# Handing rotary rotations over later, moving one table operation, and evicting the attention's values by two engines

## The chip, the cores and the metric

The kernel runs on one core of a Trainium2 chip. The metric is device microseconds of one execution. Three runs of the kernel before gave 1201.23, 1202.62 and 1203.34 us, a median of 1202.62 us. The core's engines are called PE (matrix products; its weight loads are the rows PEld), DVE (vector), ACT (scalar), POOL and SP. SP issues all transfers of this kernel, in the order in which they stand in its queue.

## The reference

The program is a two-layer encoder over 256 tokens of width 2048. Each layer normalises x, multiplies it by one wide input matrix, and feeds two groups of heads: a bidirectional recurrent scan (16 heads of 64) and an attention limited to a band of 128 tokens (16 query heads, 4 key and value heads) whose queries and keys are rotated by position. Each group is gated, the results are concatenated, multiplied by an output matrix and added to x. A last normalisation follows. The part that the change touches is the rotation, the tables for it and the values:

```python
proj = jnp.einsum('btd,dc->btc', rms_norm(x, norm_g[l]), w_in[l])
rw_in, g_rw, q, k_at, v_at, g_at = jnp.split(proj, col_splits, axis=-1)
qh, kh = rope(q, positions), rope(k_at, positions)   # t1*cos - t2*sin, t2*cos + t1*sin
y_at = window_attention(qh, kh, v_at, sink[l])        # softmax over the band and a sink
y_rw = rwkv7_branch(...)                              # one scan per direction
x = x + jnp.concatenate([y_rw * silu(g_rw), y_at * silu(g_at)], -1) @ w_out[l]
```

## The kernel before, in words

Every large product is a list of tiles of 128 output columns. A tile takes 16 **steps**, each of three products of 128x128 by 128x256 (L291 to L293), because every float32 operand is split in a high and a low part. The weights come as two halves of 512 KB per tile: SP loads one (`raw`, three buffers), ACT rounds it to the high part (`hi`, L221) and DVE subtracts that to get the low part (`lo`, L223).

The steps of all tiles stand in one queue, `Stream`. A `window` is a stretch of 64 steps (four tiles), cut in 14 slots; at chosen slots pieces of other work are put between the steps: the recurrent scan of head pairs (stages `scan_p`, `scan_i` and `scan_b`), in layer 0 the pieces of `setup` that compute the rotary tables COS and SIN, and from the eleventh window on the pieces of the attention. `S.later(n, f)` emits f when n more steps have been emitted. PE's instructions stand in exactly the order in which they are emitted. For the other engines a scheduler sets the order from dependences and priorities (`tc.high_priority` moves work forward); what is issued through `PA` and `PV` keeps its program order. Once set, each engine works through its list in order, so an instruction that waits holds back everything behind it. The helper through which `PA` and `PV` record shows as L236.

Each layer runs eight windows of scan inputs. Then, in the ninth, come 32 steps for the attention's values (`pva`, L560 to L562, two accumulators for the two halves of the tokens) and the two key tiles k0 and k1; in the tenth the query tiles q0 to q3, one after the other; in the next two the remaining four queries alternate with gate tiles. The names k0 to q7 are used below.

`rope_evac` follows every key and query tile. ACT copies the accumulator to `u` (L532). SP issues four small transfers of 32 rows (L534) that write the swapped halves to `rrot`, of which there is a single buffer. Seven steps on, `turn` gives DVE three operations: u times the cosine table, rrot times the sine table, and their sum into u. The first of these writes u, which the four transfers read, so it waits for them. Ten steps on, `parts` lets ACT write the rounded high part (from `u`) and DVE the rest.

`v_evac` scales the two accumulators of the values into `VA` with two DVE operations (L569). The accumulators stand in the two buffers that the next tiles use, so the first product of k0 waits for the first one.

The scan's triangular inverse, `scan_i`, passes between engines at each level: PE writes `pq`, ACT copies to `QF` (L900) and to `tt` (L868), PE writes `pd` (L906), DVE merges it into `tv` (L907), and PE goes on (L897, at the end L864 into `pf`). `scan_b` carries the state: PE writes `pcc` (L954 to L977), ACT evicts to `rh` (L956) and `suv` (L972), DVE scales `suv` (L979).

Of the kernel before, what the change touches and what calls it, by code (L numbers as in the profile page):

```python
# [15 lines left out]
AF = mybir.ActivationFunctionType  # L16
ALU = mybir.AluOpType
# [38 lines left out]
ROT = {0: [2, 3], 1: [], 7: [3, 6, 9], 8: [1, 4], 9: []}  # L56
PRIO_B = 95
# [76 lines left out]
def hybrid_trunk_kernel(ctx, tc, xT, wi, wv, wo, par, fing, dup, iup, sink, pos, cst, out):  # L134
    nc = tc.nc
    V, A, G, PE, SY = nc.vector, nc.scalar, nc.gpsimd, nc.tensor, nc.sync
# [22 lines left out]
    def st(tag, shape, dt=F32, bufs=1):  # L159
        return sp.tile([128, *shape], dt, tag=tag, name=tag, bufs=bufs)  # L160
# [114 lines left out]
    S = Stream()  # L275
# [117 lines left out]
    def window(n, *gens, groups=SLOTS):  # L393

        done = 0
        for i in range(groups):
            for g, at in gens:
                for _ in range(at.count(i)):
                    if g.__name__ == "scan_b":
                        with tc.high_priority(offset=PRIO_B):  # L400
                            next(g, None)
                    else:
                        next(g, None)
            upto = n * (i + 1) // groups
            S.run(upto - done)
            done = upto
# [5 lines left out]
    for l in range(DEPTH):  # L412
        L = Layer()
# [7 lines left out]
    def queue_inputs(l):  # L421
        L = layers[l]
# [100 lines left out]
        def rope_evac(place):  # L523
            def evac(pm):
                if not rope:
                    rope.extend((st("TW", [T]), st("XA", [T])))
                    V.tensor_tensor(rope[0], COS, L.norm.rb, op=ALU.mult)
                    V.tensor_tensor(rope[1], SIN, L.norm.rb, op=ALU.mult)
                CR, SR = rope
                raw = st("u", [T], bufs=2)  # L530
                rot = st("rrot", [T])
                A.activation(raw, pm, AF.Copy)  # L532
                for q in range(4):
                    SY.dma_start(out=rot[q * 32 : q * 32 + 32, :], in_=raw[(q ^ 1) * 32 : (q ^ 1) * 32 + 32, :])  # L534
                hi, lo = place()

                def turn():
                    PV.tensor_tensor(raw, raw, CR, op=ALU.mult)
                    PV.tensor_tensor(rot, rot, SR, op=ALU.mult)
                    PV.tensor_tensor(raw, raw, rot, op=ALU.add)  # L540

                def parts():
                    PA.activation(hi, raw, AF.Copy)
                    PV.tensor_tensor(lo, raw, hi.bitcast(F32), op=ALU.subtract)

                S.later(7, turn)
                S.later(10, parts)

            return evac

        pvs = []
# [13 lines left out]

        def v_evac():
            L.VA = st("VA", [2, 256])
            for b in range(2):
                V.tensor_scalar(L.VA[:, b, :], pvs[b], L.norm.rt[:, b : b + 1], None, op0=ALU.mult)  # L569

        for qt in range(4):
            S.add(
# [80 lines left out]
    def layer(l):  # L653
        L = layers[l]
# [363 lines left out]
        def scans(w):  # L1018

            gens = []  # L1020
            prep = [(w, STAGE_P0[w])] if w < 2 else [(2, STAGE_P[1]), (1, STAGE_P[0])]
            stages = [(lag, scan_p, at[0]) for lag, at in prep]
            stages += [(4, scan_b, STAGE_B[1]), (3, scan_i, STAGE_I[1]), (3, scan_b, STAGE_B[0])]
            stages += [(2, scan_i, STAGE_I[0])]
            stages += [(lag, scan_p, at[1]) for lag, at in prep]
            for lag, scan, at in stages:
                p = w - lag
                if 0 <= p < NP:
                    if (scan, p) not in chains:
                        chains[scan, p] = scan(p, L.ts[p])  # L1030
                    gens.append((chains[scan, p], at))
            return gens
# [57 lines left out]
        def attend():  # L1090

            scores(0)
            yield
            flip(0)
            scores(1)
            yield
            for j in range(8):
                values(j)
                if j < 6:
                    scores(j + 2)  # L1100
                yield
                if j < 7:
                    flip(j + 1)
                    yield

        for w in range(NP + 2):
            window(64, *scans(w), *([(setup_, ROT.get(w, [3, 6, 9, 12]))] if l == 0 else []))
        att = attend()
        window(64, *scans(NP + 2), (att, ATT[0]))
        window(64, *scans(NP + 3), (att, ATT[1]))  # L1110
# [32 lines left out]
    setup_ = setup()  # L1143
    next(setup_)
    S.run(8)
    for l in range(DEPTH):
        queue_output(l)
        if l + 1 < DEPTH:
            queue_inputs(l + 1)
        layer(l)  # L1150
        S.run(NKT * 16)
        if l + 1 < DEPTH:
            S.run(32)
# [89 lines left out]
```

## Time and profile before

| | |
|---|---|
| runs | 1201.23, 1202.62, 1203.34 us; median 1202.62 |
| profiled execution, its own time | 1201.32 us |
| its span, first to last instruction | 1199.5 us |
| PE busy / PEld busy | 1165.4 / 1087.2 us |
| DVE busy / ACT busy | 910.2 / 776.3 us |
| mean granted PE clock | 0.991 of full |
| values and k0 start in layer 0 / layer 1 | about 340 / 926 us |
| rotations in layer 0 / layer 1 | 353 to 484 / 940 to 1069 us |

How to read it. A row of waits names the engine and line that waited, what it waited for, the total in us, the number of waits and the longest. In a timeline row stand the start, the length, the engine, line and tiles, and in brackets the idle time of the engine before it and what ended that. Successive products of PE overlap, so a product shows 0.28 us while it is issued every 0.12 us. In a row of a stretch of time stand the busy time of each engine with its number of instructions, the granted PE clock, and the transfer share.

### The profile page before, as it was taken

What the parts mean: (1) busy time and instruction counts of PE and PEld (TensorE: products, weight loads), DVE (VectorE), ACT (ScalarE), POOL (GpSimd) and SP (SyncE); (2) the same over time, 40 slices, a digit from 0 to 9 for tenths busy, and PEclk for the clock granted to TensorE, in tenths of its full rate; (3) what the DMA queues carried; (4) which work ended last, traced back from release to release, by engine and by line L of the source; (5) the groups of instructions that cost most, each with busy time, mean ns of one, the idle gap of its engine ahead of it and who ended that gap; (6) DMA issues with size and microseconds to landing.
All of it is one profiled execution on the core that took longest, in us unless ns stands there. A gap on an engine that the chain in (4) does not pass through costs nothing. (4 is left out here: it accounts for less than half of the span.)

```text
span 1199.5 us, 38085 instructions
## 1 busy us (share of the span) xinstructions
PE 1165.4 (97%) x16151; PEld 1087.2 (91%) x16151; DVE 910.2 (76%) x2019; ACT 776.3 (65%) x1953; POOL 18.9 (2%) x23
## 2 busy tenths in 40 slices
PE   8999999999999999999999999999999999999996
PEld 6998999999888889999999989999998888889996
DVE  6888888888876668866667978887887766786554
ACT  6666776777776557655555766876777665665553
POOL 0000000000000000000000000000000000000000
PEclk8999999999999999999999999999999999999998
DMA  7553333323333434467655443334323333345653
GB/s 254 163 174 124 107 100 114 118 85 115 110 105 106 129 98 137 143 221 249 214 183 166 133 129 113 100 106 127 115 92 99 116 115 131 113 148 186 212 186 121
DMA packets 60410, 166.63 MB, mean 139 GB/s; under 512 B 7728, under 2 KB 22736, under 8 KB 60240
## 3 DMA queue, kind: packets, MB, share of 16 engines
q1 hardware_dynamic: 60240, 164.21, 42.5%
q8 instruction: 126, 2.06, 0.7%
q14 instruction: 44, 0.36, 0.1%
HBM read 157.37 MB, written 4.19 MB: 135 GB/s over the span
## 5 line engine op out<-in xcount | busy, mean ns | idle before, releaser
L291 PE MATMUL pm<-XH,hi 128*128 128x256 f32 x1664 | 495.9, 298 | 3.4 <-ACT XH L183 1.7
L293 PE MATMUL pm<-XH,lo 128*128 128x256 f32 x1664 | 469.9, 282 | 6.2 <-DVE lo L223 6.2
L292 PE MATMUL pm<-XL,hi 128*128 128x256 f32 x1664 | 469.4, 282 | 0.3
L221 ACT ACTIVATE hi<-raw 128x512 fp32r<-128x512 f32 x560 | 327.7, 624 | 194.9 <-PE pm L292 110.3
L223 DVE TENSOR_TENSOR lo<-raw,hi 128x512 fp32r<-128x512 f32 x560 | 369.7, 686 | 97.5 <-ACT hi L221 91.3
L291 PEld LDWEIGHTS pm<-XH,hi 128*128 128x128 f32 x1664 | 315.0, 189 | 18.5 <-ACT XH L183 2.4
L293 PEld LDWEIGHTS pm<-XH,lo 128*128 128x128 f32 x1664 | 315.4, 190 | 8.8 <-DVE lo L223 8.5
L292 PEld LDWEIGHTS pm<-XL,hi 128*128 128x128 f32 x1664 | 315.4, 190 | 1.1 <-DVE XL L184 1.1
L291 PE MATMUL pm<-MH,hi 128*128 128x256 f32 x512 | 144.1, 281 | 0.0
L293 PE MATMUL pm<-MH,lo 128*128 128x256 f32 x512 | 144.0, 281 | 0.0
L292 PE MATMUL pm<-ML,hi 128*128 128x256 f32 x512 | 143.8, 281 | 0.0
L291 PEld LDWEIGHTS pm<-MH,hi 128*128 128x128 f32 x512 | 96.6, 189 | 0.8 <-issue 0.8
L293 PEld LDWEIGHTS pm<-MH,lo 128*128 128x128 f32 x512 | 96.6, 189 | 0.2 <-DVE lo L223 0.2
L292 PEld LDWEIGHTS pm<-ML,hi 128*128 128x128 f32 x512 | 96.6, 189 | 0.0
L907 DVE CAST_PREDICATED tv<-LV,pd 128x256 f16<-128x256 uint8 x80 | 34.4, 430 | 12.8 <-PE pd L906 12.2
L790 DVE TENSOR_TENSOR ge<-pg,C 128x1024 f32<-128x1024 f32 x32 | 38.9, 1221 | 4.4 <-PE pg L784 4.4
L972 ACT ACTIVATE suv<-pcc 64x128 f32<-64x128 f32 x128 | 34.2, 267 | 11.4 <-PE pcc L970 7.1
L900 ACT ACTIVATE QF<-pq 128x256 f16<-128x256 f32 x80 | 30.8, 384 | 14.3 <-PE pq L864 13.8
L1062 ACT ACTIVATE mv<-mv,mx 128x257 f32<-128x257 f32 x64 | 31.8, 501 | 11.3 <-DVE mx L1059 11.3
L956 ACT ACTIVATE rh<-pcc 128x128 f32<-128x128 f32 x64 | 17.5, 273 | 33.2 <-PE pcc L954 32.8
L784 PE MATMUL pg<-mv,bk 64*128 64x128 f32 x512 | 37.2, 285 | 0.3 <-DVE ge L790 0.3
L784 PEld LDWEIGHTS pg<-mv,bk 64*128 64x128 f32 x512 | 31.1, 187 | 2.4 <-DVE ge L790 0.4
(247 smaller groups left out, 1860.1 us busy)
## 6 DMA issues: line engine op xcount, KB each, us to landing
raw<-wi SPq DMA_DIRECT2D x207, 512.0 KB, 3.8
raw<-wo SPq DMA_DIRECT2D x64, 512.0 KB, 4.2
raw<-wv SPq DMA_DIRECT2D x8, 512.0 KB, 3.7
rrot<-u SPq DMA_DIRECT2D x80, 32.0 KB, 2.1
vg<-xT SPq DMA_DIRECT2D x16, 128.0 KB, 4.2
xd<-vg SPq DMA_DIRECT2D x16, 128.0 KB, 3.5
vg<-xd SPq DMA_DIRECT2D x16, 128.0 KB, 3.7
g<-dup SPq DMA_DIRECT2D x16, 97.0 KB
```

What stands on the lines that cost most here:

```text
L221: A.activation(hi[:, q], raw[:, q], AF.Copy)
L223: V.tensor_tensor(lo[:, q], raw[:, q], hi[:, q].bitcast(F32), op=ALU.subtract)
L291: PE.matmul(pm, wh, rh[:, kk, :], start=(kk == 0), stop=False)
L292: PE.matmul(pm, wh, rl[:, kk, :], start=False, stop=False)
L293: PE.matmul(pm, wl, rh[:, kk, :], start=False, stop=(kk == 15))
L784: PE.matmul(pg[:, h, c * 128 : (c + 1) * 128], BK[half[h], d, c, 1 - h : 3 - h, :].rearrange("p s j -> p (s j)"), MV[half[h], d, c].rearra ...
L790: V.tensor_tensor(GEd(d), pg.rearrange("p h (c x) -> p h c x", c=NC), gm[d].unsqueeze(1).unsqueeze(1).to_broadcast([128, 2, NC, 128]), op= ...
L900: A.activation(t_sub(QF), flat4(pq[:, :, 0:128]), AF.Copy)
L907: V.copy_predicated(t_sub(TC), t_mask, flat4(pd[:, :, 0:128]))
L956: A.activation(RH, pc[:, 0], AF.Copy)
L972: A.activation(here(h), pc[half[h], 1], AF.Copy)
L1062: A.activation(Sc[:, h, q, 0:257], Sc[:, h, q, 0:257], AF.Exp, scale=0.125, bias=mx[:, q : q + 1], accum_out=den[:, q : q + 1])
```

## The change

Three places are edited. The rotation of a tile is handed over 13 steps after its eviction instead of 7, and its rounding 15 steps after instead of 10. In the third to the seventh window of layer 0, the third of four pieces of `setup` moves from slot 9 to slot 12, where the fourth stands as well. `v_evac` gives the first accumulator to ACT and the second to DVE, both at raised priority.

```diff
-                S.later(7, turn)
-                S.later(10, parts)
+                S.later(13, turn)
+                S.later(15, parts)
...
         def v_evac():
             L.VA = st("VA", [2, 256])
-            for b in range(2):
-                V.tensor_scalar(L.VA[:, b, :], pvs[b], L.norm.rt[:, b : b + 1], None, op0=ALU.mult)
+            with tc.high_priority(offset=PRIO_B):
+                A.activation(L.VA[:, 0, :], pvs[0], AF.Copy, scale=L.norm.rt[:, 0:1])
+                V.tensor_scalar(L.VA[:, 1, :], pvs[1], L.norm.rt[:, 1:2], None, op0=ALU.mult)
...
         for w in range(NP + 2):
-            window(64, *scans(w), *([(setup_, ROT.get(w, [3, 6, 9, 12]))] if l == 0 else []))
+            window(64, *scans(w), *([(setup_, ROT.get(w, [3, 6, 12, 12]))] if l == 0 else []))
```

The order of PE's instructions and of POOL's is the same before and after; the orders of DVE, ACT and SP differ. One line is added in `v_evac`, so lines behind it count one more in the kernel after (L907 becomes L908).

The first place is DVE in the tenth window of layer 0, where q0 and q1 are rotated (`u` and `rrot` with the tables, which lie in `TW` and `XA`). Before:

```order
L907 COPY_PREDICATED tv<-LV,pd 128x2x64x2
L236 TENSOR_TENSOR u<-u,TW 128x256
L236 TENSOR_TENSOR rrot<-rrot,XA 128x256
L223 TENSOR_TENSOR lo<-raw,hi 128x512
L236 TENSOR_TENSOR u<-u,rrot 128x256
L979 TENSOR_TENSOR suv<-pcc,pc 64x2x64 x2
L236 TENSOR_TENSOR iu<-u,kr 128x256
L223 TENSOR_TENSOR lo<-raw,hi 128x512 x2
L907 COPY_PREDICATED tv<-LV,pd 128x2x32x4
```

and after:

```order
L908 COPY_PREDICATED tv<-LV,pd 128x2x64x2
L223 TENSOR_TENSOR lo<-raw,hi 128x512 x2
L980 TENSOR_TENSOR suv<-pcc,pc 64x2x64 x2
L236 TENSOR_TENSOR u<-u,TW 128x256
L236 TENSOR_TENSOR rrot<-rrot,XA 128x256
L236 TENSOR_TENSOR u<-u,rrot 128x256
L236 TENSOR_TENSOR iu<-u,kr 128x256
L223 TENSOR_TENSOR lo<-raw,hi 128x512
L908 COPY_PREDICATED tv<-LV,pd 128x2x32x4
```

Two of the low parts and the scaling of `suv` now stand ahead of the rotation of q0, and the low part of the query (`iu`) directly behind it.

The second place is ACT where the values end in layer 0. Before:

```order
L236 ACTIVATE pp<-lw 128x512
L956 ACTIVATE rh<-pcc 128x128
L236 ACTIVATE ip<-lw 128x512
```

and after:

```order
L236 ACTIVATE pp<-lw 128x512
L569 ACTIVATE VA<-pva,rt 128x256
L957 ACTIVATE rh<-pcc 128x128
L236 ACTIVATE ip<-lw 128x512
```

The eviction of the first accumulator stands on ACT between `pp` and `rh`; on DVE one of the two evictions is gone and the other keeps its place behind the reciprocal of `kd`.

The third place is SP's queue at the transfers of q0. The first row ends with what it waits for; before it is

```order
L534 DMA rrot_7367<-u_7366 32x256 [waits DMAHW3_49,DMAHW2_49,DMAHW4_49,DMAHW1_49,Activation_49]
L534 DMA rrot_7367<-u_7366 32x256 [waits DMAHW0_49]
L534 DMA rrot_7367<-u_7366 32x256 x2
L213 DMA raw_7757<-wi 128x1024 [waits DVE_49]
```

and after

```order
L534 DMA rrot_7367<-u_7366 32x256 [waits DMAHW2_49,DMAHW3_49,DMAHW1_49,DMAHW4_49,DVE_49,Activation_49]
L534 DMA rrot_7367<-u_7366 32x256 [waits DMAHW0_49]
L534 DMA rrot_7367<-u_7366 32x256 x2
L213 DMA raw_7757<-wi 128x1024 [waits DVE_49]
```

The first transfer of the tile now waits for DVE as well: the rotation of the tile before must have read the single `rrot`. A weight load stands behind it.

## The prediction

> **What bounds the kernel now.** I read the page's busy times first, then the waits of PE, then the timelines at the places where PE waited.
>
> ```profile
> PE 1165.4 (97%) x16151; PEld 1087.2 (91%) x16151; DVE 910.2 (76%) x2019; ACT 776.3 (65%) x1953; POOL 18.9 (2%) x23
> ```
>
> PE works nearly throughout and keeps its instruction order, so a change can only give what PE now loses. These are its longest waits over the whole run:
>
> ```profile
> PE pm L293 <- DVE lo L223: 6.2, 11, 1.2
> PE pq L897 <- DVE tv L907: 3.5, 8, 0.8
> PE pf L864 <- DVE tv L907: 3.1, 5, 1.5
> PE pcc L977 <- ACT suv L972: 2.7, 2, 1.8
> PE pd L906 <- ACT tt L868: 1.9, 2, 1.0
> PE pm L291 <- DVE VA L569: 1.3, 2, 0.7
> ```
>
> Except for the first, they lie mostly where the keys and queries are rotated. The waits of DVE and ACT over the run say why:
>
> ```profile
> DVE u L236 <- DMA rrot<-u: 17.9, 10, 3.2
> ACT kr L236 <- DVE u L236: 12.7, 10, 3.0
> ```
>
> In 10 of 20 rotations DVE stands still until the four transfers have landed, and ACT behind it in its copy `kr` of the rotated tile. Both work through their lists in order, so what PE needs next is stuck. The timeline of q0 in layer 0 shows it:
>
> ```profile
> 376.06 0.38 ACT L532 ACTIVATE u<-pm 128x256 f32<-128x256 f32 x1
> 376.47 2.64 SPq L534 DMA_DIRECT2D rrot<-u  x4
> 381.57 0.43 DVE L236 TENSOR_TENSOR u<-u,TW 128x256 f32<-128x256 f32 x1 [2.04 <-DMA rrot<-u]
> 383.30 0.42 ACT L236 ACTIVATE kr<-u 128x256 fp32r<-128x256 f32 x1 [2.29 <-DVE u L236]
> 384.98 0.38 ACT L868 ACTIVATE tt<-pq 128x256 f16<-128x256 f32 x1
> 385.41 0.30 PE L906 MATMUL pd<-QF,tt 64*64 64x32 f16 x16 [1.03 <-ACT tt L868]
> 386.08 0.37 ACT L532 ACTIVATE u<-pm 128x256 f32<-128x256 f32 x1
> ```
>
> From the eviction (376.06) to the rotation (381.57) pass 5.5 us, because SP alone needs 2.64 us to issue four transfers. DVE has idled 2.04 us by then, ACT 2.29, and PE pays 1.03 for a late `tt`. The next tile pays through DVE:
>
> ```profile
> 390.73 0.42 DVE L236 TENSOR_TENSOR u<-u,TW 128x256 f32<-128x256 f32 x1 [2.94 <-DMA rrot<-u]
> 393.56 0.42 DVE L907 CAST_PREDICATED tv<-LV,pd 128x256 f16<-128x256 uint8 x1
> 394.04 0.30 PE L897 MATMUL pq<-tv,AB 64*64 64x32 f16 x16 [0.81 <-DVE tv L907]
> ```
>
> **The later hand-over.** A tile is 16 steps: 386.08 less 376.06 is 10.02 us, 9.0 without PE's wait of 1.03 in it, so 0.56 us a step. Seven steps are 3.9 us, less than the 5.5 that the transfers took; thirteen are 7.3 us, 1.8 more than they took. The wait on the transfers should vanish in the tenth window; where gates and attention lie between, a step is longer still and the room larger. Nothing is removed: the same three operations, copy, subtraction and four transfers are issued.
>
> What PE gets back: of the waits on `tv`, `suv` and `tt` above, 3.5 + 3.1 + 2.7 + 1.9 = 11.2 us, the scans without rotation take 1.5 (from 60 to 330 us) and 0.4 (from 625 to 915 us), by these two rows:
>
> ```profile
> PE pq L897 <- DVE tv L907: 1.5, 5, 0.6
> ...
> PE pq L897 <- DVE tv L907: 0.4, 1, 0.4
> ```
>
> That leaves 9.3 us. Pieces of 0.2 are common and I leave three of them in place: **8.7 us**, bounds 0 (another wait takes over each time) and 9.3.
>
> **The clock.** The longest stall costs twice. In layer 0 ACT's `suv` came late behind `kr` (first rows), and the granted clock fell right after:
>
> ```profile
> 411.05 0.42 ACT L236 ACTIVATE kr<-u 128x256 fp32r<-128x256 f32 x1 [2.96 <-DVE u L236]
> 412.41 0.54 ACT L972 ACTIVATE suv<-pcc 64x128 f32<-64x128 f32 x2
> ...
> 413.01 0.45 PE L977 MATMUL pcc<-suv,bt 128*64 128x64 f32 x8 [1.78 <-ACT suv L972]
> 417.68 0.29 PE L1047 MATMUL pscr<-KA,iu 64*128 64x256 f32 x2
> ...
> 410.00:415.00 5.00, 3.22 (x34) 2.94 (x33) 3.77 (x10) 2.31 (x6) 0.00 (x0) 0.87 0.10 16
> 415.00:420.00 5.00, 5.00 (x44) 4.44 (x43) 3.91 (x14) 1.96 (x5) 0.00 (x0) 0.79 0.53 179
> ...
> 997.58 0.45 PE L977 MATMUL pcc<-suv,bt 128*64 128x64 f32 x8 [0.93 <-ACT suv L972]
> 1000.76 0.28 PE L1047 MATMUL pscr<-KA,iu 64*128 64x256 f32 x2
> ```
>
> The third number from the right in the two rows of stretches is the clock: 0.87 and 0.79. The same work of PE, from L977 to the scores' L1047, took 417.68 - 413.01 = 4.67 us there and 1000.76 - 997.58 = 3.18 us in layer 1, where the stall was 0.93 and no clock was lost. The difference, **1.5 us**, comes back if the stall goes; bounds 0 and 1.5.
>
> The Trainium skill, "TensorE: Matmul & The Clock Gate", Part 1, speaks against this term: it has the clock fall to half only after at least one idle window of about 3.4 us, free-running, and 1.78 us is no such window. By it the drop would not be due to this stall, and the sum below would be 1.5 us smaller. The trace shows the drop behind a stall of half that length.
>
> **The values.** In layer 0, at 343 us (the first row below is of all 20 evictions of such a tile by ACT):
>
> ```profile
> L532 ACT ACTIVATE u<-pm x20: 361/366/383, 353.5 to 1060.0; 128x256 f32<-128x256 f32 x20
> ...
> 342.89 0.28 ACT L956 ACTIVATE rh<-pcc 128x128 f32<-128x128 f32 x1 [1.18 <-PE pcc L954]
> 343.31 0.38 DVE L569 TENSOR_SCALAR VA<-pva,rt 128x256 f32<-128x256 f32 x1
> 343.75 0.39 PE L291 MATMUL pm<-XH,hi 128*128 128x256 f32 x1 [0.66 <-DVE VA L569]
> ```
>
> DVE reaches the first eviction at 343.31, and k0's first product waits 0.66 us for it. ACT idled 1.18 us until 342.89; it can take the accumulator there, for some 0.37 us, and PE would find it free at about 343. `rh` behind it slips by at most that. I count the whole wait, **1.3 us** for both layers; bounds 0 (ACT is held by something else) and 1.3. The second accumulator is needed only by k1, 16 steps on.
>
> **The table piece.** In the third to seventh window DVE is dense and a table operation delays `tv`; in the fifth:
>
> ```profile
> 144.01 0.42 DVE L236 SCALAR_TENSOR_TENSOR VA<-VA 128x256 f32<-128x256 f32 x1
> 148.13 0.30 PE L897 MATMUL pq<-tv,AB 64*64 64x32 f16 x16 [0.23 <-DVE tv L907]
> ```
>
> PE waits for `tv` 1.5 us there in layer 0 and 0.4 in layer 1, where no tables are computed. Moved to slot 12, the operation stands beside `ysq`, behind these merges. Gain **1.1 us**, the difference; bounds 0 and 1.5.
>
> **What it may cost.** The rotation is now late where the transfers were. DVE needs three operations and PE's next eviction is three steps (1.7 us) on:
>
> ```profile
> L236 DVE TENSOR_TENSOR rrot<-rrot,XA x20: 416/419/421, 359.2 to 1067.3; 128x256 f32<-128x256 f32 x20
> 464.00:500.00 36.00, 36.00 (x314) 32.51 (x313) 30.67 (x101) 24.29 (x68) 0.00 (x0) 1.00 0.43 139
> ```
>
> Three times 0.42 is 1.3 us, a little less than 1.7. Three things queue behind it. SP's next four transfers now wait for it, and a weight load behind them. The low part of the tile (`iu`) stands directly behind the rotation on DVE and waits for ACT's copy, with `lo` and `tv` behind. And in the attention, where DVE is busy 30.67 of 36 us, eight rotations move onto the scores' operations. The nearest row for a new PE wait is the one on `lo`: 6.2 us in 11, 0.56 each. With 20 rotations the bounds are 0 and 11.2 us. Since DVE has its idle time in the tenth window to catch up in, and PE has no wait at all from 464 to 500 us, I take four: **2.2 us**.
>
> **The sum.** 8.7 + 1.5 + 1.3 + 1.1 - 2.2 = 10.4 us off the profiled execution's 1201.32 us gives 1190.9. The median of the runs is 1202.62, 1.3 above that execution; since medians are compared, I predict 1192.2 us.
>
> **The rivals.**
>
> Half of it goes into a new wait: `iu` waits on DVE for ACT's copy at every tile, and `tv` behind it. For it speaks that the low part has moved up against the rotation; against it that the copy takes 0.42 us, not the 2 to 3 us of the transfers. With ten new waits of 0.56, 5.6 us, the sum is 12.6 - 5.6 = 7.0, and if the clock's 1.5 is not won either, 5.5: about 1197.1.
>
> The clock drop is not due to the stall but to a fixed point of a window of its own, as the rule above would have it. All else as forecast, the gain is 8.9: 1193.7. For it: a stall of 1.78 us is short; against it: in the other layer, at the same work and half the stall, nothing fell.
>
> The change does nothing that counts: DVE is held just as long by something else, since scans, weights and rotations share it. The waits only change names, 12.6 is lost to 20 waits of 0.6, and the time is about 1202.0. Against it: DVE is idle in the waits, not working.
>
> Slower: the single `rrot`. SP may not issue the next tile's transfers before DVE has read it; if DVE is behind by more than the 0.4 us that 1.7 leaves over 1.3, SP blocks, weight loads behind it come late, and PE waits in L293 at every tile. It decides from 12.6 / 20 = 0.63 us a tile on; at 0.8 us it is 16 us lost, 3.4 more than was won: 1206.0. For it: five tiles in each layer follow each other without a gate between. Against it: with gates between, a tile has 32 steps, so half the tiles have room.
>
> **How the numbers follow.** Forecast 0.57; half of it 0.17; the clock as the rule has it 0.12; nothing 0.08; slower 0.06. The likeliest gives 1192.2. With new waits 0 and all bounds won, 9.3 + 1.5 + 1.3 + 1.5 = 13.6 us, it is 1189.0, and some of the 6.2 us on `lo` may go too, so the range begins at 1188.0. Upwards it takes in the half (1197.1) and reaches to 1200.2, where a gain can just be told: a measurement of this kernel tells about 0.2%, 2.4 us, from no change. Faster: 0.57 + 0.17 + 0.12 less a little for halves that come out smaller, 0.84; within: 0.09; slower: 0.07.
>
> **What would show it.** In the profile of the changed kernel the wait of DVE's `u` on `rrot` should be below 2 us in total (17.9 now), that of ACT's `kr` on DVE below 5 (12.7 now), PE's waits on `suv` and `tt` between the rotations gone, the clock full between 400 and 430 us, no wait of L291 on VA, and PE's wait on `tv` in the third to seventh window below 0.6. New waits of PE on `lo` of more than 4 us beyond the 6.2, or SP waiting for DVE's rotation ahead of L534 for more than 1 us a tile, would make the prediction wrong. It is also wrong if these waits vanish and the time does not follow, since then PE's waits were not what the kernel lost.

## The result, and the profile after

The changed kernel took 1190.54 us (median of four runs, 1189.04 to 1191.54) beside 1201.95 us for the kernel before: a ratio of 0.9903, 95% interval 0.9885 to 0.9920, or 11.7 us faster (9.6 to 13.8). A second comparison gave 0.9912 (0.9897 to 0.9928). Of all the executions behind this and the ratios below, one is not counted: the kernel with eight transfers at 13 steps once took 1241.64 us at a mean granted clock of 0.846. The forecast was 1192.2 us in a range from 1188.0 to 1200.2.

The page of the changed kernel:

```profile
span 1189.7 us, 38093 instructions
...
PE 1164.0 (98%) x16151; PEld 1084.4 (91%) x16151; DVE 908.2 (76%) x2017; ACT 777.7 (65%) x1955; POOL 18.7 (2%) x23
```

All engines are as busy as before, within 3 us, and the span is 9.8 us shorter: 1.4 us are PE's busy time, 8.4 are time in which PE did nothing (34.1 us before, 25.7 now). Work was not saved, waits were. PE's waits over the run (lines behind 570 count one more than before):

```profile
PE pm L293 <- DVE lo L223: 6.4, 12, 1.2
PE pq L898 <- DVE tv L908: 1.7, 5, 0.6
...
PE pf L865 <- DVE tv L908: 0.7, 3, 0.2
PE pm L291 <- DVE VA L570: 0.7, 1, 0.7
...
PE pn L929 <- ACT tt L869: 0.4, 2, 0.2
```

The waits on `suv` (2.7 us before) and on `tt` ahead of `pd` (1.9) are gone, those on `tv` fell from 6.6 to 2.4, and the one on VA halved. The waits of DVE and ACT at the rotations:

```profile
DVE u L236 <- DMA rrot<-u: 4.9, 4, 2.6
...
ACT kr L236 <- DVE u L236: 4.5, 7, 0.9
```

They were 17.9 and 12.7 us. The timeline of q0 in layer 0, as it was shown of before:

```profile
375.23 0.39 ACT L532 ACTIVATE u<-pm 128x256 f32<-128x256 f32 x1
375.64 2.42 SPq L534 DMA_DIRECT2D rrot<-u  x4
381.53 0.42 DVE L236 TENSOR_TENSOR u<-u,TW 128x256 f32<-128x256 f32 x1
381.56 0.38 ACT L869 ACTIVATE tt<-pq 128x256 f16<-128x256 f32 x1
382.79 0.42 ACT L236 ACTIVATE kr<-u 128x256 fp32r<-128x256 f32 x1 [0.85 <-DVE u L236]
383.42 0.30 PE L907 MATMUL pd<-QF,tt 64*64 64x32 f16 x16
383.79 0.37 ACT L532 ACTIVATE u<-pm 128x256 f32<-128x256 f32 x1
```

The rotation starts 6.3 us after the eviction, where it started 5.5 us after, but without a wait. ACT now writes `tt` ahead of `kr` and not behind it, and PE goes from one product to the next without the 1.03 us. The tile takes 8.56 us, 375.23 to 383.79, instead of 10.02.

### The profile page after: what moved, and what is told of

Its sections match the earlier page's. It is cut to its first block, busy times and chain, and to the rows that moved or that the text cites. A ratio compares the mean times of both kernels' runs of the same rounds, so it can differ in the third digit from the quotient of the medians.

```text
span 1189.7 us, 38093 instructions
## 1 busy us (share of the span) xinstructions
PE 1164.0 (98%) x16151; PEld 1084.4 (91%) x16151; DVE 908.2 (76%) x2017; ACT 777.7 (65%) x1955; POOL 18.7 (2%) x23
## 4 chain that ended last, share of the span: by engine, by line
PE 71%; issue 15%; DVE 7%; DMA 3%; ACT 2%; POOL 1%; SPq 0%; DVEq 0%; POOLq 0%; ACTq 0%
PE pm L291 18%; PE pm L293 15%; PE pm L292 15%; PE pg L785 3%; DMA raw<-wi 3%; DVE lo L223 2%; PE pcc L955 2%; PE py L985 2%; PE py L962 1%; PE pcc L978 1%; PE pq L898 1%; PE pcc L968 1%; PE pd L907 1%; PE pza L670 1%; DVE kd L236 1%
## 5 line engine op out<-in xcount | busy, mean ns | idle before, releaser
L291 PE MATMUL pm<-XH,hi 128*128 128x256 f32 x1664 | 494.4, 297 | 2.4 <-ACT hi L221 0.9
L291 PEld LDWEIGHTS pm<-XH,hi 128*128 128x128 f32 x1664 | 313.5, 188 | 18.1 <-ACT XH L183 1.9
L291 PE MATMUL pm<-MH,hi 128*128 128x256 f32 x512 | 144.1, 281 | 0.0
L291 PEld LDWEIGHTS pm<-MH,hi 128*128 128x128 f32 x512 | 96.6, 189 | 1.0 <-issue 0.8
L908 DVE CAST_PREDICATED tv<-LV,pd 128x256 f16<-128x256 uint8 x80 | 34.3, 429 | 12.1 <-PE pd L907 11.5
L957 ACT ACTIVATE rh<-pcc 128x128 f32<-128x128 f32 x64 | 17.5, 274 | 34.1 <-PE pcc L955 33.7
L980 DVE TENSOR_TENSOR suv<-pcc,pc 64x128 f32<-64x128 f32 x96 | 27.4, 286 | 7.6 <-PE pcc L978 6.8
```

Source lines behind the costliest of these rows:

```text
L291: PE.matmul(pm, wh, rh[:, kk, :], start=(kk == 0), stop=False)
L908: V.copy_predicated(t_sub(TC), t_mask, flat4(pd[:, :, 0:128]))
L980: V.tensor_tensor(here(h, i + 1), pS[half[h]], pick(PC, half[h], i, [2 * NC - 1 - 2 * i, 2], [0, 64]), op=ALU.mult)
```

## The experiments

Each kernel was compared with the kernel before, run beside it on the same chip. The median of before lay between 1199.9 and 1200.5 us in these comparisons, with single runs from 1197.8 to 1203.0; ratios of one comparison tell some 0.1 to 0.2%, that is 1 to 2 us.

| kernel | ratio to before | 95% interval |
|---|---|---|
| rotation alone | 0.9906 | 0.9892 to 0.9921 |
| values alone | 1.0003 | 0.9992 to 1.0015 |
| table piece alone | 1.0005 | 0.9994 to 1.0016 |
| rotation and values, no table piece | 0.9900; again 0.9906 | 0.9887 to 0.9913; 0.9891 to 0.9921 |
| rotation, both values by ACT | 0.9901 | 0.9885 to 0.9917 |
| changed kernel again | 0.9912 | 0.9897 to 0.9928 |
| no transfers, hand-over at 7 | 0.9925 | 0.9910 to 0.9940 |
| hand-over at 10 and 13 | 0.9959 | 0.9945 to 0.9973 |
| eight transfers, hand-over at 7 | 1.0074 | 1.0057 to 1.0091 |
| eight transfers, hand-over at 13 | 1.0006 | 0.9996 to 1.0016 |

### The three parts, each alone

The rotation alone:

```diff
-                S.later(7, turn)
-                S.later(10, parts)
+                S.later(13, turn)
+                S.later(15, parts)
```

> Only the later hand-over (13 and 15 steps), values and table as before. Theory: the waits of DVE on the four transfers were what PE lost at the rotations, so nearly all of the gain is here: PE's waits on tv, suv and tt between the rotations gone (9 us), no half clock at 400 to 430 us (1.5 us), 10 us faster than the kernel before, about 1191.5 us. Rival (three parts share the gain): 5 to 7 us faster, 1195 to 1197 us.

It took 1189.01 us beside 1200.02, 11.0 us less. Its waits of DVE on the transfers and of PE on `tv`:

```profile
DVE u L236 <- DMA rrot<-u: 5.1, 5, 2.3
...
PE pq L897 <- DVE tv L907: 1.9, 6, 0.6
```

The 1.9 us are those that the scans without rotation had before (1.5 and 0.4). PE's waits on `suv` and on `pf` are gone, the clock stays full where it had fallen, at 410 to 420 us, and the two waits on VA remain. All of the gain that the times can tell is in this part.

The values alone:

```diff
-            for b in range(2):
-                V.tensor_scalar(L.VA[:, b, :], pvs[b], L.norm.rt[:, b : b + 1], None, op0=ALU.mult)
+            with tc.high_priority(offset=PRIO_B):
+                A.activation(L.VA[:, 0, :], pvs[0], AF.Copy, scale=L.norm.rt[:, 0:1])
+                V.tensor_scalar(L.VA[:, 1, :], pvs[1], L.norm.rt[:, 1:2], None, op0=ALU.mult)
```

> Only the values evicted by ACT and DVE. Theory: in layer 1 k0's first product waits for ACT and no longer, in layer 0 it stands in the buffer of the second accumulator and still waits 0.7 us for DVE; 0.7 us faster than before, about 1201.2 us. Rival (the prediction's term): 1.3 us faster, the wait gone in both layers. The stalls of the rotations stay, so this run also tells of the clock: if the half clock at 410 to 420 us follows from the 1.8 us stall, it is there again; if it was chance, it is not there, or elsewhere.

No difference can be told: the interval reaches to 1.0 us faster, which leaves room for the expected 0.7 and just none for 1.3. The wait itself can be read: 0.7 us in layer 0, none in layer 1. In the changed kernel the place in layer 0 is

```profile
342.85 0.47 ACT L569 ACTIVATE VA<-pva,rt 128x256 f32<-128x256 f32 x1 [0.43 <-PE pva L562]
...
344.01 0.38 DVE L570 TENSOR_SCALAR VA<-pva,rt 128x256 f32<-128x256 f32 x1
...
344.44 0.39 PE L291 MATMUL pm<-XH,hi 128*128 128x256 f32 x1 [0.66 <-DVE VA L570]
```

ACT was done at 343.32, in good time, but k0 starts only behind DVE's eviction of the second accumulator, which stands behind DVE's reciprocal. In layer 1 it starts ahead of that eviction, at 923.70 against 924.00. So in layer 0 of this program k0 must have been given the second accumulator's buffer, and in layer 1 the first one's; the rows do not name the buffers.

The table piece alone:

```diff
-            window(64, *scans(w), *([(setup_, ROT.get(w, [3, 6, 9, 12]))] if l == 0 else []))
+            window(64, *scans(w), *([(setup_, ROT.get(w, [3, 6, 12, 12]))] if l == 0 else []))
```

> Only the table piece moved from slot 9 to slot 12. Theory from the profile after: the wait on tv that it was to free is set by ACT's hi, and the operation now delays the last tv ahead of pf; 0.7 us slower than before, about 1202.6 us, with PE's wait on tv from 60 to 330 us near 1.3 and on pf 0.7. Rival (the prediction's term): 1.1 us faster, tv below 0.6. The clock: as in the run of the values alone.

The ratio tells nothing either way; the forecast gain of 1.1 us is just outside of the interval, which ends at 0.7 us faster. PE's waits from 60 to 330 us in this kernel:

```profile
PE pq L897 <- DVE tv L907: 1.3, 4, 0.6
PE pf L864 <- DVE tv L907: 0.7, 3, 0.3
```

They were 1.5 and nothing. The changed kernel shows why `tv` is no earlier, in the fifth window, where the table operation is gone from 144 us:

```profile
145.15 0.42 DVE L433 TENSOR_TENSOR u<-pm,rb 128x256 f32<-128x256 f32 x1
145.98 1.29 DVE L223 TENSOR_TENSOR lo<-raw,hi 128x512 fp32r<-128x512 f32 x2 [0.42 <-ACT hi L221]
...
147.59 0.42 DVE L908 CAST_PREDICATED tv<-LV,pd 128x256 f16<-128x256 uint8 x1
...
148.06 0.30 PE L898 MATMUL pq<-tv,AB 64*64 64x32 f16 x16 [0.23 <-DVE tv L908]
```

DVE gets to its low parts 0.42 us early and waits for ACT's high part. The time that the operation took is now idle: `tv` comes at 147.59 and PE waits 0.23 us for it, as before. Put into slot 12, the operation stands ahead of the level's last `tv`; that this is what `pf` now waits for is inferred from the order and from the new waits.

The changed kernel without the table piece, twice, the second time beside the changed kernel:

> The changed kernel with the table piece back at slot 9. Theory: 0.7 us faster than the changed kernel, 12 us faster than before, about 1189.8 us. Rival (the table piece gains): 1 us slower than the changed kernel, 1191.6 us.

> The changed kernel with the table piece back at slot 9, again, beside the changed kernel on one chip. Theory: 0.7 us faster than it. Rival: the same or slower.

> The changed kernel again, beside the one without the moved table piece. Theory: 11 us faster than before and 0.7 us slower than its neighbour.

1188.20 us the first time, 1188.84 the second, beside 1189.95 for the changed kernel: the sign is the expected one, and the intervals overlap. From waits alone the table piece costs some 0.5 us; the measured times do not settle it.

Both halves of the values by ACT, with the later rotation and without the table piece:

```diff
+            with tc.high_priority(offset=PRIO_B):
+                for b in range(2):
+                    A.activation(L.VA[:, b, :], pvs[b], AF.Copy, scale=L.norm.rt[:, b : b + 1])
```

> Later hand-over as in the changed kernel, table piece as before, and both halves of the values evicted by ACT at the raised priority. Theory: PE's wait on VA, which the change kept in layer 0 (0.7 us, because k0 got the accumulator that DVE evicts), is gone in both layers; 1.3 us less than with the rotation alone, 12.3 us faster than before. Rival: the second eviction on ACT holds back rh and suv and costs what it wins; as fast as the rotation alone.

No wait on VA is left in its profile, and `rh` behind the two evictions cost PE nothing there. With 1188.84 us it is the kernel with the fewest PE waits; it cannot be told from its neighbours by time.

### The transfers

Without them, at the early hand-over:

```diff
-                for q in range(4):
-                    SY.dma_start(out=rot[q * 32 : q * 32 + 32, :], in_=raw[(q ^ 1) * 32 : (q ^ 1) * 32 + 32, :])
...
-                    PV.tensor_tensor(rot, rot, SR, op=ALU.mult)
+                    PV.tensor_tensor(rot, raw, SR, op=ALU.mult)
```

> The kernel before, hand-over at 7 and 10 steps, but without the four transfers: rrot is made from u times the sine table without swapping the halves, so the rotation is left incomplete and 80 transfers are left out. Theory: what PE lost at the rotations is DVE's wait for the transfers and nothing else; without them the early hand-over is as good as the late one: 10 to 11 us faster than before, about 1190 us, no wait of u on rrot, no half clock at 415 us. Rival (the early place on DVE itself is what costs, ahead of tv and suv): at most 4 us faster, and PE keeps its waits on tv and suv there.

The kernel leaves the swap of the halves out. It took 1190.98 us beside 1200.51: 9.5 us less, with the hand-over still at 7 and 10 steps. PE keeps 0.8 us on `pf`, while ACT still waits for the rotation:

```profile
PE pf L862 <- DVE tv L905: 0.8, 2, 0.4
...
ACT kr L236 <- DVE u L236: 9.1, 6, 2.7
```

The rotation did not stand later on DVE for it. The scheduler put that of q0 even ahead of `tv`, behind which it stood before:

```profile
377.94 0.42 DVE L236 TENSOR_TENSOR u<-u,TW 128x256 f32<-128x256 f32 x1
...
379.19 0.45 DVE L905 CAST_PREDICATED tv<-LV,pd 128x256 f16<-128x256 uint8 x1
```

So the early place alone costs little, and the waits for the transfers nearly all; the 1.5 us between this kernel and the rotation alone are within the noise of the two ratios. That 80 transfers less stand in SP's queue is no sign of a gain of its own: PE's wait on `lo` is 6.4 us, as in the changed kernel. ACT's long waits for DVE at this place did not reach PE.

The hand-over at 10 and 13 steps:

```diff
-                S.later(7, turn)
-                S.later(10, parts)
+                S.later(10, turn)
+                S.later(13, parts)
```

> The kernel before with the hand-over at 10 and 13 steps. Theory (5.5 us from eviction to landed transfers, 0.56 us a step, so 9.8 steps): ten steps are just about enough in the tenth window, DVE's wait on rrot falls from 18 to 3 to 8 us and at least three quarters of the gain are there: 8 to 11 us faster, 1190 to 1193 us. Rival (it takes 13 for other reasons, such as the place of the rotation against tv): under 5 us faster.

Less than expected: 4.9 us faster (3.2 to 6.6), about what the rival had. DVE waits longer for the transfers than before the change, and PE loses half as much:

```profile
DVE u L236 <- DMA rrot<-u: 23.6, 12, 3.7
...
PE pt L807 <- DVE ge L790: 1.9, 2, 1.4
...
367.40 0.43 DVE L236 TENSOR_TENSOR u<-u,TW 128x256 f32<-128x256 f32 x1 [2.47 <-DMA rrot<-u]
...
369.41 1.22 DVE L790 TENSOR_TENSOR ge<-pg,C 128x1024 f32<-128x1024 f32 x1
...
370.69 0.46 PE L807 MATMUL pt<-C,vg 64*64 64x64 f32 x16 [1.39 <-DVE ge L790]
...
382.13 0.43 DVE L236 TENSOR_TENSOR u<-u,TW 128x256 f32<-128x256 f32 x1 [2.13 <-DMA rrot<-u]
382.81 0.38 ACT L868 ACTIVATE tt<-pq 128x256 f16<-128x256 f32 x1
383.86 0.42 ACT L236 ACTIVATE kr<-u 128x256 fp32r<-128x256 f32 x1 [0.67 <-DVE u L236]
```

At k1 the rotation was put ahead of `ge`, which PE needs. At q0 (evicted at 376.18) DVE reaches the rotation 3.8 us after the eviction and waits 2.13 us, where it was 3.5 and 2.04 before; at q1 it is 1.9 and 3.66 us, where it was 1.7 and 2.94. So three steps more hardly moved the rotation in DVE's list: a number of steps is a place in the program, and DVE runs ahead of PE. What did move is ACT's copy: `tt` now stands ahead of `kr`, and PE no longer pays at q0. PE's waits on ACT's `suv` and `tt` (4.6 us before) are gone and the clock stays full, while those on `tv` fell only from 6.6 to 4.3, and 1.9 on `ge` and 0.8 on DVE's `suv` are new. Behind the 3.66 us at q1 PE lost 0.9. The total that DVE waits says little; what counts is the instruction next in the list, on DVE and on ACT. The expectation had taken steps for time since the eviction.

Eight transfers of 16 rows in place of four of 32, at both hand-overs:

```diff
                 for q in range(4):
-                    SY.dma_start(out=rot[q * 32 : q * 32 + 32, :], in_=raw[(q ^ 1) * 32 : (q ^ 1) * 32 + 32, :])
+                    for h in (0, 16):
+                        o, i = q * 32 + h, (q ^ 1) * 32 + h
+                        SY.dma_start(out=rot[o : o + 16, :], in_=raw[i : i + 16, :])
```

> The kernel before with each swap of halves issued as eight transfers of 16 rows instead of four of 32; 7 and 10 steps. SP's issue goes from 2.5 to about 5 us. Theory: each of the waits of DVE grows by some 2.5 us and all 20 rotations wait, 60 us or more in total instead of 18; PE pays a good part of it: 20 to 40 us slower than before, and the clock falls to half at more than one place. Rival (transfers hidden, only the place on DVE counts): within 3 us of before.

> Eight transfers of 16 rows with the hand-over at 13 and 15 steps, nothing else changed against the kernel before. Theory: 5.5 + 2.5 = 8.0 us from eviction to landing against 7.3 us of 13 steps: the waits of DVE return in the tenth window at under 1 us each, 10 to 15 us in total, and SP's longer issue delays weights a little: 3 to 8 us faster than before, 1192 to 1197 us, and far ahead of the same eight at 7 steps. Rival: as at 7 steps, slower than before.

At 7 steps it is 8.9 us slower than before (6.8 to 10.9), where 20 to 40 were expected; at 13 steps the same as before, where 3 to 8 us faster were expected. At the same eight transfers the later hand-over is worth about 8 us. SP's issue at 7 steps, and the waits of ACT and DVE:

```profile
377.80 6.11 SPq L536 DMA_DIRECT2D rrot<-u  x8
...
DVE u L236 <- DMA rrot<-u: 22.5, 13, 3.5
...
ACT kr L236 <- DVE u L236: 24.1, 9, 4.2
```

The first expectation took the order for fixed. With longer transfers the scheduler put the rotation of q0 behind two low parts and `suv`, as the change does, and DVE's total rose to 22.5 us only. At 13 steps:

```profile
384.12 5.57 SPq L536 DMA_DIRECT2D rrot<-u  x8
...
392.74 0.42 DVE L236 TENSOR_TENSOR u<-u,TW 128x256 f32<-128x256 f32 x1 [3.55 <-DMA rrot<-u]
...
394.47 0.42 ACT L236 ACTIVATE kr<-u 128x256 fp32r<-128x256 f32 x1 [3.16 <-DVE u L236]
...
396.19 0.55 ACT L974 ACTIVATE suv<-pcc 64x128 f32<-64x128 f32 x2
...
396.50 0.68 PE L986 MATMUL py<-suv,ge 128*64 128x64 f32 x7 [1.60 <-ACT suv L974]
```

q1 was evicted at 383.73. SP begins to issue 0.4 us later but needs 5.57 us, and the last transfer lands when DVE has waited 3.55 us, 9.0 us after the eviction; ACT's copy waits with it, and `suv` behind. The slower rival of the prediction is not what is seen here: SP waits for DVE ahead of 8 tiles, 9.7 us in all, but did so for 8.7 in the changed kernel, and PE's wait on `lo` is 6.7 us, beside 6.4 there. PE's new waits (3.0 us on `suv`, 1.9 on `tt`) and two stretches at half clock, at some 1.5 us each, make 7.9 of the some 12 us that lie between this kernel and the rotation alone. The rest was not traced.

### The clock

> The kernel with the rotation alone, and in layer 1 behind the state's eviction rh of six head pairs 8, 12, 16, 20, 24 and 28 copies of it in place on ACT, so that PE stalls there for growing times of about 0 to 5 us; the result is the same. Theory on the clock: a stall of about 1.8 us or more is followed by 3.4 us at half clock when it falls into one of the clock's windows, shorter ones are not; so the later stalls have half clock behind them and the first ones none. Rival (a whole idle window of 3.4 us is needed): only the stalls over 3.4 us are followed by half clock.

```diff
                 A.activation(RH, pc[:, 0], AF.Copy)
+                if l == 1 and i == 1:
+                    for _ in range({1: 8, 2: 12, 3: 16, 4: 20, 5: 24, 6: 28}.get(p, 0)):
+                        A.activation(RH, RH, AF.Copy)
                 yield
```

This kernel was run once, in 1234.30 us. The stalls were longer than meant: 1.04, 3.68, 5.00, 6.36, 7.78 and 9.50 us, from 8 copies to 28. The rows of the first two, with the stretches around them:

```profile
752.09 0.45 PE L970 MATMUL pcc<-rh,vf 64*64 64x64 f32 x8 [1.04 <-ACT rh L959]
797.13 0.45 PE L970 MATMUL pcc<-rh,vf 64*64 64x64 f32 x8 [3.68 <-ACT rh L959]
...
750.00:760.00 10.00, 8.96 (x158) 8.20 (x156) 7.70 (x16) 8.57 (x26) 0.00 (x0) 1.00 0.23 88
796.00:804.00 8.00, 6.87 (x105) 6.61 (x106) 4.80 (x10) 4.03 (x12) 0.00 (x0) 0.79 0.01 2
```

The third number from the right is the clock: full at the first stall, fallen behind the second. The run leaves open what happens between 1.04 and 3.68 us, but the other kernels have stalls there. The values alone and the table piece alone kept the stalls of before, and lost the clock at the same place again; in the values alone:

```profile
414.30 0.45 PE L978 MATMUL pcc<-suv,bt 128*64 128x64 f32 x8 [1.96 <-ACT suv L973]
...
415.00:420.00 5.00, 5.00 (x38) 4.53 (x39) 3.23 (x9) 1.74 (x4) 0.00 (x0) 0.66 0.42 125
```

No kernel whose rotation comes without such stalls lost it there. In every trace the granted clock changes at whole multiples of 3.413 us from its first change. Laid over the stalls, this grid gives the following; the first 20 us and the end of each execution, where the clock changes too, are left out:

| kernel | stall, us | most of it in one cell of the grid, us | half clock behind it |
|---|---|---|---|
| table piece alone | 2.03 | 1.99 | yes |
| values alone | 1.96 | 1.96 | yes |
| eight at 7 | 1.92 | 1.92 | yes |
| eight at 13 | 1.88 | 1.88 | yes |
| before | 1.78 | 1.78 | yes |
| eight at 13 | 1.60 | 1.60 | yes |
| eight at 7 | 1.70 | 1.70 | no |
| eight at 7 | 2.33 | 1.63 | no |
| eight at 7 | 1.86 | 1.61 | no |
| eight at 7 | 1.59 | 1.59 | no |
| values alone | 1.58 | 1.58 | no |
| table piece alone | 1.50 | 1.50 | no |
| before | 1.47 | 1.47 | no |

So about half a cell of idle time in one cell is enough, and a longer stall that straddles two cells passes. The stall of 3.68 us agrees: 1.11 us of it lie in one cell and 2.57 in the next, so no cell was idle throughout, and the clock fell. The exact limit, and why 1.60 us fell once while 1.70 did not, stays open. The grid does not keep its place: two profiled executions of the changed kernel have it 0.5 us apart. So the same stall may lose the clock in one execution and not in another, and how often it did so before was not measured.

The Trainium skill, "TensorE: Matmul & The Clock Gate", Part 1, has a free-running window of 3413 ns; the grid agrees. It has the clock fall after at least one idle window; here 1.78 to 1.99 us within one were enough.

## Why the prediction was right

**The bound.** Right: PE's waits were what the kernel lost. PE's work is unchanged, and the span fell by what PE waited less, 8.4 us, and by 1.4 us of busy time.

**The later hand-over, 8.7 us of at most 9.3.** Right in size: the waits on `tv`, `suv` and `tt` at the rotations are gone in both layers, leaving 0.4 us on `tt` ahead of `pn`, so 8.9 came back. With the clock's 1.5 us that makes 10.4, and the rotation alone gained 11.0 (9.5 to 13.0). That it was the waits for the transfers, and not the early place on DVE by itself, is shown by the kernel without them: 9.5 us at the early hand-over.

The reckoning in time was weaker than the size. Steps are places in the program. Seven steps were put at 3.9 us, and DVE stood at q1's rotation 1.7 us after the eviction; ten would be 5.6 us, and it stood there after 1.9. At thirteen it came after 6.3 us at q0 and 6.4 at q1, because low parts and `suv` now stand ahead, so the wait vanished in the tenth window as forecast. In the eleventh there was no margin at all: DVE was ready for q3's rotation 3.1 us after the eviction (402.15) and waited,

```profile
407.83 0.43 DVE L236 TENSOR_TENSOR u<-u,TW 128x256 f32<-128x256 f32 x1 [2.56 <-DMA rrot<-u]
```

yet PE lost nothing behind it. The prediction had steps there longer than in the tenth window; they took 0.56 us in both, by the evictions of q0, q3 and q4 (375.23, 402.15 and 420.14, 48 and 32 steps).

**The clock, 1.5 us.** Right for the profiled executions, and the doubt against it is answered: the drop followed the stall in all three kernels that kept it, and in none that lost it. In the medians the term can be smaller, since a stall of 1.78 us can also fall across two cells; the times do not tell 1.5 us.

**The values, 1.3 us.** Half right. The statement that failed is that only k1 needs the second accumulator: in layer 0 of the changed kernel k0 waits for it. The wait of 0.7 us there stayed, and with both evictions on ACT it goes.

**The table piece, 1.1 us.** Wrong in sign by the waits; the times do not tell it. The difference between the layers was read as the table operation's price. The operation was there, but ACT's high parts, one step behind, set the time, and at its new place it seems to hold up another `tv`: the waits grew by 0.5 us.

**New waits, 2.2 us.** They did not come. SP did begin to wait for DVE ahead of the transfers, in the changed kernel as in the rotation alone,

```profile
SPq L534 <- DVE u L236: 8.7, 8, 1.3
```

but no weight came late for it: PE's wait on `lo` is 6.4 us, beside 6.2. The low parts of rotated queries on DVE (`iu`, and `du` for the next tile) wait for ACT's copy, as the first rival had it, but only four times and for 2.7 us in all, and PE does not wait behind them. The attention's dense stretch took the rotations without a new PE wait.

The three misses, 0.7 of the values, 1.6 of the table piece and 2.2 of the new waits, almost cancel. That is luck: the sum of 10.4 is nearer to the measured 11.7 than its terms deserve.

**The signs.** The waits on `suv` and on `tt` ahead of `pd` went, the clock stayed full, and ACT's wait of 4.5 us was below 5. Three signs were missed: DVE waited 4.9 us for the transfers and not below 2, L291 still waited for VA, and PE's waits on `tv` in the windows with tables are 1.3 and 0.7 us, not below 0.6. One sign against the prediction was met in part: SP's waits are 1.1 us each, above the limit of 1, but in 8 tiles of 20, and they cost PE nothing.

## What to carry to other kernels

When an engine that works in order waits for a transfer, price the instruction next behind it, not the wait: 23.6 us of waiting cost less than 17.9 did. Hand over work that depends on a transfer after its measured landing, and check in the built order where each engine then stands: a number of steps is not a time, and a scheduler can answer a longer transfer with another order by itself. Two layers that differ in one operation show where a wait is, but not that the operation causes it; look for the next input that would be waited for.

## What the runs showed of the hardware that was not expected

A PE stall of 1.78 us was followed by 3.41 us at half clock, when it lay in one cell of a grid of 3.413 us, and cost 1.5 us on top; one of 2.33 us that lay across two cells was not. SP took 4.9 to 6.3 us to issue eight transfers of 16 KB, beside 2.4 to 3.4 us for four of 32 KB; the median of one was 0.59 us at both sizes, so here the number of transfers set the time and not their size.
